# Reading the activations of a two-part float32 product in turn from four places

## The chip, the cores and the metric

The kernel runs on one core of one Trainium2 chip. The metric is the device time of one execution in microseconds (us). The kernel before takes 2208.91 us, the median of three runs (2207.38 to 2209.27).

## The reference

One inference step of a one-layer decoder trunk for a prompt of 256 tokens and 8 samples of 4 tokens, 288 tokens in all, of width 2048, in float32. Cut to what matters here:

```python
def swiglu(x, w_in, w_out):
    gate, up = jnp.split(x @ w_in, 2, axis=-1)
    return (jax.nn.silu(gate) * up) @ w_out
...
x = x + 0.5 * rmsnorm(swiglu(rmsnorm(x, g[0]), ffn1_w_in[l], ffn1_w_out[l]), g[1])
m, sg, sh = hybrid_mixer(rmsnorm(x, g[2]), mix_w_in[l], ...)   # merged @ mix_w_out inside
x = x + rmsnorm(m, g[3])
x = x + 0.5 * rmsnorm(swiglu(rmsnorm(x, g[4]), ffn2_w_in[l], ffn2_w_out[l]), g[5])
```

The FFNs are 5632 wide. The mixer projects its input to the operands of two groups of gated recurrences (GLA with 4 heads, HGRN2 with 8), runs them over chunks with exact causality, and projects the gated, normalised outputs back. Nearly all of the arithmetic is in products of the 288 tokens with the weight matrices.

## The kernel before

**Layout.** Everything is kept with features on the 128 partitions and the 288 tokens along the free axis, so x is 16 tiles of 128 x 288. A weight product holds a 128 x 128 slice of weights in TensorE and streams the 288 columns of an x tile past it into a PSUM tile.

**Two parts.** A float32 value is kept as a high part, which is the value rounded to the type `float32r` that TensorE multiplies in one pass, and a low part, which is the rest. A product of two values is then three products of parts: high x high, low x high and high x low. That is `mm3` in `block` (line 587 on): line 596 streams the high part of the activations past the high part of the weights, line 597 streams the low part past the same high slice, and line 598 streams the high part again past the low slice. All three add up in one PSUM tile. The helper that makes a matmul also makes the load of its slice of weights, so every product has a load of its own, line 597's too.

**The weights.** `Weights` (line 41 on) streams them. A unit is 512 KB, 128 x 1024 numbers: two rows of 128 features by 512 columns (in some products four by 256). `load` (line 65) issues its DMA on SyncE's queue into one of three `raw` buffers. `pieces` (line 86 on) splits it: ScalarE copies it to the high part (line 100), VectorE subtracts to get the low part (line 101). Both parts of a unit lie in one `wh` tile of two rows. A row holds 512 high numbers, then 512 low ones, then 32 numbers that nobody uses: `HALF` is 1024 + 32. Four such buffers (and two more at the borders between sub-layers) let the split run ahead of TensorE. `ahead` and `next` do this by counting; there is no planner.

**The loops.** `block` computes 512 (or 256) output features, as 4 PSUM tiles (`f`). It takes the units one after the other, and for each unit goes over `f`, over the unit's rows `k`, and over the three products. In some blocks at the beginnings of sub-layers (`byk`, `late`, `fill`) the order is by `k` first, with the products of the low part of the activations put later, because those parts are made while the block runs. TensorE executes in the order written.

**The activations' parts.** Those of x are `xh[k]` and `xl[k]` (lines 251 and 252), 32 tiles of 128 x 288. They are written by `split_to` (line 261): ScalarE writes the high part with a gain (line 262), VectorE the low part (line 263). The mixer writes its gated outputs into the same tiles in `split_y` (line 1637). At the two borders between sub-layers, `Fill` (line 513 on) has tiles of its own for the first four `k`, so that the next block's first products can begin before the norm is known.

In an FFN, `do_in` (line 667) computes a chunk of 512 hidden features: gate, up, and the activated product `u`. `ev_up` (line 689) writes the parts of `u` into `hh` and `hl`, two tiles of 128 x 4 x 288 each with two buffers (lines 693 and 694). `do_out` multiplies them with the second matrix; its `block` asks for `[t[:, k % 4, :] for t in hs[k // 4]]` (line 801). A result is read from PSUM by VectorE or ScalarE in the order of the tokens.

**Order around the change.** Engines wait for each other by semaphores that the framework derives from the tiles which instructions write and read. In a few places an order is written by hand with `tc.issue_after` and `order`, mostly at the borders: the post-norm's updates of x (line 566 on), the splits that follow each of them, and the first products that use them.

Of the kernel before, what the change touches and what calls it, by code (L numbers as in the profile page):

```python
# [9 lines left out]
F32 = mybir.dt.float32  # L10
F32R = mybir.dt.float32r
U8 = mybir.dt.uint8
AF = mybir.ActivationFunctionType
ALU = mybir.AluOpType
PSUM = bass.MemoryType.PSUM

P = 128
TP = 256
TS = 32
T = TP + TS  # L20
# [3 lines left out]
KT = D // P  # L24
# [8 lines left out]
HL_BUFS = 4  # L33
HALF = 1024 + 32
SCAN_LAG = 4
# [95 lines left out]
def trunk_kernel(ctx, tc, x_prompt, x_sample, state_gla, state_hgrn, norm_gains, f1_in, f1_out, f2_in, f2_out,  # L131
# [3 lines left out]
    V, S, G, PE = nc.vector, nc.scalar, nc.gpsimd, nc.tensor  # L135

    const = ctx.enter_context(tc.tile_pool(name="const", bufs=1))
    xpool = ctx.enter_context(tc.tile_pool(name="xpool", bufs=1))
# [108 lines left out]
    EARLY = 4  # L247
    x = [xpool.tile([P, T], F32, name=f"x{k}") for k in range(KT)]
    yg = [xpool.tile([P, 4, T], F32, name=f"y{k}") for k in range(4)]
    y = [yg[k // 4][:, k % 4, :] for k in range(KT)]  # L250
    xh = [xpool.tile([P, T], F32R, name=f"xh{k}") for k in range(KT)]
    xl = [xpool.tile([P, T], F32R, name=f"xl{k}") for k in range(KT)]
    rt = xpool.tile([P, T], F32, name="rt")
# [6 lines left out]

    def split_to(parts, src, col):
        i1 = S.activation(parts[0], src, AF.Copy, scale=col).ins
        i2 = V.scalar_tensor_tensor(parts[1], src, col, parts[0].bitcast(F32), op0=ALU.mult, op1=ALU.subtract).ins
        return i1, i2
# [246 lines left out]
    class Fill:  # L511
# [3 lines left out]
        def __init__(self, pool, name, gains, gnext, some, ahead):  # L515
            self.gnext, self.name, self.some, self.ahead = gnext, name, some, ahead

            tiles = [[[pool.tile([P, T], F32R, name=f"{name}{n}{p}{k}") for k in range(EARLY)] for p in "hl"] for n in "xy"]
            self.tiles = [list(zip(*hl)) for hl in tiles]
            self.gains = pool.tile([P, 48], F32, name=f"{name}g")[:, 0:EARLY]  # L520
            V.tensor_tensor(self.gains, gains[:, 0:EARLY], prm[:, gnext * KT:gnext * KT + EARLY], op=ALU.mult)
# [65 lines left out]
    def block(name, nk, rhs, evac, width=512, tick=None, tail=1, hold=False, most=99, fill=None, late=0, byk=(), lag=0, skip=()):  # L587
# [6 lines left out]
        def mm3(dst, w, f, k, parts, start, stop):  # L594
            a, c = k % per, slice(f * P, f * P + P)
            yield lambda: PE.matmul(dst, w[0][:, a, c], parts[0], start=start, stop=False)  # L596
            yield lambda: PE.matmul(dst, w[0][:, a, c], parts[1], start=False, stop=False)  # L597
            yield lambda: PE.matmul(dst, w[1][:, a, c], parts[0], start=False, stop=stop)  # L598
# [60 lines left out]
    def ffn(tag, gcol, gnext, pn, before, fill=None):  # L659
# [3 lines left out]
        with ExitStack() as pools:  # L663
# [3 lines left out]
            def do_in(c):  # L667
                hh = fp.tile([P, 4, T], F32R, name=f"hh{tag}_{c}", tag="hh")
                hl = fp.tile([P, 4, T], F32R, name=f"hl{tag}_{c}", tag="hl")
                hid[c] = (hh, hl)  # L670
# [18 lines left out]
                def ev_up(f, ps):  # L689
                    u = fp.tile([P, T], F32, name="u", tag="u", bufs=3)  # L690
                    ins = V.tensor_tensor(u, ps, rt, op=ALU.mult).ins  # L691
                    V.tensor_tensor(u, u, gs[f], op=ALU.mult)
                    S.activation(hh[:, f, :], u, AF.Copy)
                    V.tensor_tensor(hl[:, f, :], u, hh[:, f, :].bitcast(F32), op=ALU.subtract)
                    return ins
# [63 lines left out]
            def do_out(c, n):  # L759
                hs = [hid.pop(c + i) for i in range(n)]  # L760
# [7 lines left out]
                for o in range(4):  # L768
                    def ev(f, ps):
# [17 lines left out]
                        if end:  # L787
                            if not final:
                                border[0].fill.new(k)
                            elif k < KT - 1:  # L790
# [6 lines left out]
                                else:  # L797
                                    if f > 1:
                                        by_token(zs[f - 2], k - 2, *zt)
                                    zs.append(z)  # L800
                    block(f"out{tag}_{c}_{o}", 4 * n, lambda k: [t[:, k % 4, :] for t in hs[k // 4]], ev,
                          tail=2 if end and o == 3 else 1, hold=end and o == 3)
# [97 lines left out]
    def mixer(pn, border):  # L900
        with ExitStack() as mx:
# [735 lines left out]
            def split_y(t):  # L1637
                S.activation(xh[t], y[t], AF.Copy)
                V.tensor_tensor(xl[t], y[t], xh[t].bitcast(F32), op=ALU.subtract)

# [92 lines left out]
```

## Time and profile before

| What | Value |
|---|---|
| median of three runs | 2208.91 us |
| span of the profiled execution | 2206.5 us |
| TensorE busy, instructions | 2198.2 us, 17828 |
| VectorE busy | 1385.7 us (63%) |
| ScalarE busy | 1020.1 us (46%) |
| read from memory, written | 363.75 MB, 11.80 MB |
| mean rate of all transfers | 174 GB/s |

The profile is of one execution. PE is TensorE's matmuls, PEld its loads of weights, DVE is VectorE, ACT ScalarE, POOL GpSimd and SP SyncE, whose queue issues most DMAs. The span runs from the first to the last instruction of the program; the runs' times are of the whole execution. A group's row gives its line, engine, operation, what it writes and reads, its form and count, then the busy time, the mean duration in ns, and the time its engine sat idle just before, with what ended that. Matmuls are pipelined and their ends are modelled, so durations of neighbours overlap; their starts are recorded.

### The profile page before, as it was taken

To read this page: it belongs to the slowest core of one execution; us is meant where nothing else is said; L and a number is where in the kernel's file an instruction comes from. 1 tells how busy PE (TensorE), PEld (TensorE's weight loads), DVE (VectorE), ACT (ScalarE), POOL (GpSimd) and SP (SyncE) were. 2 spreads that over 40 slices of the span, in tenths; PEclk is the share of its full clock that TensorE was granted. 3 is DMA by queue.
4 is the path that set the end of the run, shared out by engine and by line. 5 is a ranking of instruction groups with operands and counts; after the bars stand their busy time and mean duration, and the time that the engine had idled before them with its cause. 6 is when DMAs were issued, how large, how long until landed. Compare 5 with 4: busy or idle time off the path is not lost.

```text
span 2206.5 us, 43225 instructions
## 1 busy us (share of the span) xinstructions
PE 2198.2 (100%) x17828; PEld 2182.2 (99%) x17828; DVE 1385.7 (63%) x2253; ACT 1020.1 (46%) x1537; POOL 180.0 (8%) x327
## 2 busy tenths in 40 slices
PE   9999999999999999999999999999999999999998
PEld 9999999999999999999999999999999999999998
DVE  7545546555555568888888755844555466556646
ACT  6443433343344345655676654543333333333344
POOL 2000000000000001233210000000000020122005
PEclk9999999999999999999999999999999999999999
DMA  7655555555555554667566564555555565666555
GB/s 223 174 166 171 169 168 170 171 165 171 172 166 180 179 166 142 194 207 216 173 189 176 176 190 135 169 167 171 171 166 170 172 176 172 180 179 179 172 164 161
DMA packets 227334, 384.87 MB, mean 174 GB/s; under 512 B 21362, under 2 KB 60864, under 8 KB 227136
## 3 DMA queue, kind: packets, MB, share of 16 engines
q1 hardware_dynamic: 213872, 365.02, 55.1%
q0 software_dynamic: 10992, 16.77, 2.8%
q8 instruction: 140, 2.29, 0.4%
q10 hardware_dynamic: 2272, 0.31, 0.1%
q14 instruction: 58, 0.48, 0.1%
HBM read 363.75 MB, written 11.80 MB: 170 GB/s over the span
## 4 chain that ended last, share of the span: by engine, by line
PE 98%; DVE 1%; ACT 1%; issue 0%; POOL 0%; DVEq 0%; ACTq 0%; POOLq 0%
PE gate L597 10%; PE gate L596 10%; PE gate L598 10%; PE up L597 8%; PE out L597 8%; PE up L596 8%; PE up L598 8%; PE out L596 8%; PE out L598 8%; PE hfq L596 2%; PE hfq L597 2%; PE mo L597 2%; PE hfq L598 2%; PE mo L596 1%; PE mo L598 1%; PE hi L597 1%
## 5 line engine op out<-in xcount | busy, mean ns | idle before, releaser
L101 DVE TENSOR_TENSOR wh<-raw,wh 128x1024 fp32r<-128x1024 f32 (+1 forms) x676 | 821.7, 1217 | 610.2 <-ACT wh L100 609.1
L100 ACT ACTIVATE wh<-raw 128x1024 fp32r<-128x1024 f32 (+1 forms) x676 | 711.0, 1053 | 943.1 <-PE gate L598 295.2
L597 PE MATMUL gate<-xl,wh 128*128 128x288 f32 x1660 | 490.1, 297 | 0.0
L598 PE MATMUL gate<-xh,wh 128*128 128x288 f32 x1660 | 483.6, 293 | 0.0
L596 PE MATMUL gate<-xh,wh 128*128 128x288 f32 x1660 | 483.0, 292 | 0.0
L597 PE MATMUL out<-hl,wh 128*128 128x288 f32 x1408 | 419.2, 298 | 0.0
L597 PE MATMUL up<-xl,wh 128*128 128x288 f32 x1408 | 419.2, 298 | 0.0
L598 PE MATMUL up<-xh,wh 128*128 128x288 f32 x1408 | 411.6, 292 | 0.0
L598 PE MATMUL out<-hh,wh 128*128 128x288 f32 x1408 | 411.5, 292 | 0.0
L596 PE MATMUL out<-hh,wh 128*128 128x288 f32 x1408 | 409.3, 291 | 0.0
L596 PE MATMUL up<-xh,wh 128*128 128x288 f32 x1408 | 409.3, 291 | 0.0
L596 PEld LDWEIGHTS gate<-xh,wh 128*128 128x128 f32 x1660 | 313.7, 189 | 0.8 <-DVE u L691 0.4
L598 PEld LDWEIGHTS gate<-xh,wh 128*128 128x128 f32 x1660 | 311.4, 188 | 0.2 <-DVE wh L101 0.2
L597 PEld LDWEIGHTS gate<-xl,wh 128*128 128x128 f32 x1660 | 310.2, 188 | 0.5
L596 PEld LDWEIGHTS out<-hh,wh 128*128 128x128 f32 x1408 | 266.8, 189 | 0.2 <-DVE y L782 0.2
L596 PEld LDWEIGHTS up<-xh,wh 128*128 128x128 f32 x1408 | 266.7, 189 | 0.0
L598 PEld LDWEIGHTS up<-xh,wh 128*128 128x128 f32 x1408 | 264.5, 188 | 0.0
L598 PEld LDWEIGHTS out<-hh,wh 128*128 128x128 f32 x1408 | 264.5, 188 | 0.0
L597 PEld LDWEIGHTS up<-xl,wh 128*128 128x128 f32 x1408 | 263.8, 187 | 0.0
L597 PEld LDWEIGHTS out<-hl,wh 128*128 128x128 f32 x1408 | 263.7, 187 | 0.0
L782 DVE TENSOR_TENSOR y<-out,y 128x288 f32<-128x288 f32 x287 | 120.7, 452 | 82.1 <-PE out L598 81.1
L739 POOL DMA_DIRECT2D xT<-b x64 | 37.1, 586 | 757.3 <-PE gate L598 566.7
(417 smaller groups left out, 2559.1 us busy)
## 6 DMA issues: line engine op xcount, KB each, us to landing
raw<-in_ffn_w_in_dram SPq DMA_DIRECT2D x350, 512.0 KB, 3.6
raw<-in_ffn_w_out_dram SPq DMA_DIRECT2D x176, 512.0 KB, 3.6
raw<-in_mix_w_in_dram SPq DMA_DIRECT2D x64, 512.0 KB, 4.3
raw<-in_mix_w_in_dram SPq DMA_DIRECT2D x96, 256.0 KB, 3.2
raw<-in_mix_w_out_dram SPq DMA_DIRECT2D x32, 512.0 KB, 3.7
out_dram<-s POOLq DMA_DIRECT2D x32, 256.0 KB, 2.9
s<-in_state_gla_dram SPq DMA_DIRECT2D x16, 256.0 KB, 5.9
s<-in_state_hgrn_dram SPq DMA_DIRECT2D x16, 256.0 KB, 5.6
```

What stands on the lines that cost most here:

```text
L100: i1 = self.nc.scalar.activation(h[:, a, c], raw[:, a, c], AF.Copy).ins
L101: i2 = self.nc.vector.tensor_tensor(l[:, a, c], raw[:, a, c], h[:, a, c].bitcast(F32), op=ALU.subtract).ins
L596: yield lambda: PE.matmul(dst, w[0][:, a, c], parts[0], start=start, stop=False)
L597: yield lambda: PE.matmul(dst, w[0][:, a, c], parts[1], start=False, stop=False)
L598: yield lambda: PE.matmul(dst, w[1][:, a, c], parts[0], start=False, stop=stop)
L739: queues[n % len(queues)].dma_start(dst[q * TS:(q + 1) * TS, 4 * g:4 * g + 4, :, cols].rearrange("p k t c -> p (k t) c"), b32[rows, q])
L782: V.tensor_tensor(y[k], ps, y[k], op=ALU.add)
```

## The change

The high and the low part of an activation tile now share one tile, made by a new function `pair`: 4 groups, in each group 72 high numbers and then 72 low ones. A group is a quarter of the tokens. `xh`, `xl`, the tiles of `Fill`, and `hh` and `hl` of an FFN chunk (now one tile `hp` of 4 such pairs) are views of these. Writers put the parts in through a view of the source in four groups (`columns`). In `mm3` both the streamed part and the PSUM tile are viewed through `turns_of`: the stream takes columns 0 to 3 of group 0, then 0 to 3 of group 1, of group 2, of group 3, then columns 4 to 7 of each, and so on for 18 rounds. A token's result still lands in the PSUM column of that token, so whatever reads PSUM is as before. The 32 unused numbers at the end of a row of `wh` go away.

```diff
-HALF = 1024 + 32
+HALF = 1024
+LINE = 4
+PLACES = 4
+
+
+def columns(t):
+
+    return t.rearrange("p (g c) -> p g c", g=PLACES)
+
+
+def turns_of(t):
+
+    return t.rearrange("p g (i e) -> p i g e", e=LINE)
+
+
+def pair(pool, name):
+
+    t = pool.tile([P, PLACES, 2, T // PLACES], F32R, name=name)
+    return t[:, :, 0, :], t[:, :, 1, :]
...
-    xh = [xpool.tile([P, T], F32R, name=f"xh{k}") for k in range(KT)]
-    xl = [xpool.tile([P, T], F32R, name=f"xl{k}") for k in range(KT)]
+    xh, xl = zip(*(pair(xpool, f"xp{k}") for k in range(KT)))
...
     def split_to(parts, src, col):
+        src = columns(src)
         i1 = S.activation(parts[0], src, AF.Copy, scale=col).ins
...
-            tiles = [[[pool.tile([P, T], F32R, name=f"{name}{n}{p}{k}") for k in range(EARLY)] for p in "hl"] for n in "xy"]
-            self.tiles = [list(zip(*hl)) for hl in tiles]
+            self.tiles = [[pair(pool, f"{name}{n}{k}") for k in range(EARLY)] for n in "xy"]
...
             a, c = k % per, slice(f * P, f * P + P)
+            dst, parts = turns_of(columns(dst)), [turns_of(t) for t in parts]
             yield lambda: PE.matmul(dst, w[0][:, a, c], parts[0], start=start, stop=False)
...
-                hh = fp.tile([P, 4, T], F32R, name=f"hh{tag}_{c}", tag="hh")
-                hl = fp.tile([P, 4, T], F32R, name=f"hl{tag}_{c}", tag="hl")
+                hp = fp.tile([P, 4, PLACES, 2, T // PLACES], F32R, name=f"hp{tag}_{c}", tag="hp")
+                hh, hl = ([hp[:, f, :, j, :] for f in range(4)] for j in range(2))
...
-                    S.activation(hh[:, f, :], u, AF.Copy)
-                    V.tensor_tensor(hl[:, f, :], u, hh[:, f, :].bitcast(F32), op=ALU.subtract)
+                    S.activation(hh[f], columns(u), AF.Copy)
+                    V.tensor_tensor(hl[f], columns(u), hh[f].bitcast(F32), op=ALU.subtract)
...
-                    block(f"out{tag}_{c}_{o}", 4 * n, lambda k: [t[:, k % 4, :] for t in hs[k // 4]], ev,
+                    block(f"out{tag}_{c}_{o}", 4 * n, lambda k: [t[k % 4] for t in hs[k // 4]], ev,
...
-                S.activation(xh[t], y[t], AF.Copy)
-                V.tensor_tensor(xl[t], y[t], xh[t].bitcast(F32), op=ALU.subtract)
+                S.activation(xh[t], columns(y[t]), AF.Copy)
+                V.tensor_tensor(xl[t], columns(y[t]), xh[t].bitcast(F32), op=ALU.subtract)
```

## The prediction

> **What bounds the kernel now.** I read the page first: the busy line, the granted clock and the chain that ended last.
>
> ```profile
> span 2206.5 us, 43225 instructions
> PE 2198.2 (100%) x17828; PEld 2182.2 (99%) x17828; DVE 1385.7 (63%) x2253; ACT 1020.1 (46%) x1537; POOL 180.0 (8%) x327
> PEclk9999999999999999999999999999999999999999
> PE 98%; DVE 1%; ACT 1%; issue 0%; POOL 0%; DVEq 0%; ACTq 0%; POOLq 0%
> ```
>
> TensorE is never out of work and its clock is granted in full; 98% of the chain is matmuls. Ends of matmuls overlap, so "100%" says only that there is always one in flight. What counts is how fast they follow each other. I take that from the busy time by stages, and for each of the three lines that issue a product (`hi x hi` L596, `lo x hi` L597, `hi x lo` L598) over the whole span and in the mixer. The columns are: stage, its length, TensorE busy (count), weight loads busy (count), then, where they are given, VectorE and ScalarE.
>
> ```profile
> 100.00:300.00 200.00, 200.00 (x1541) 200.00 (x1540) 106.67 (x141) 81.43 (x101) 0.00 (x0) 1.00 0.56 169
> 800.00:1300.00 500.00, 499.42 (x4813) 487.16 (x4812) 411.15 (x860) 307.33 (x627) 88.94 (x158) 1.00 0.63 184
> 1500.00:2150.00 650.00, 650.00 (x5003) 650.00 (x5002) 363.76 (x513) 249.36 (x282) 45.85 (x80) 1.00 0.57 172
> 0.00:2207.00 2207.00, 1568.05 (x5384) 1018.15 (x5384) 1.00 0.58 174
> 0.00:2207.00 2207.00, 1594.82 (x5384) 1007.35 (x5384) 1.00 0.58 174
> 0.00:2207.00 2207.00, 1572.69 (x5384) 1011.01 (x5384) 1.00 0.58 174
> 800.00:1300.00 500.00, 318.40 (x1083) 203.84 (x1083) 1.00 0.63 184
> ```
>
> In an FFN stretch a matmul starts every 650/5003 = 0.130 us. There are 3 x 5384 = 16152 products of 288 columns; at 130 ns they fill 2100 us of the span's 2206.5, so 1 ns on each is 16.2 us, or 0.73%. Of the products, 3 x 1083 = 3249 lie in the mixer stage (800 to 1300 us), the only long one where VectorE is also close to full (411 of 500 us); 12903 lie elsewhere.
>
> Next, whether the three products are alike. First the page's groups (count, busy, mean ns of one, idle before), then the order in time (start, duration), in two places because starts are rounded to 10 ns.
>
> ```profile
> L597 PE MATMUL out<-hl,wh 128*128 128x288 f32 x1408 | 419.2, 298 | 0.0
> L598 PE MATMUL out<-hh,wh 128*128 128x288 f32 x1408 | 411.5, 292 | 0.0
> L596 PE MATMUL out<-hh,wh 128*128 128x288 f32 x1408 | 409.3, 291 | 0.0
> ```
>
> ```profile
> 1417.64 0.29 PE L596 MATMUL up<-xh,wh 128*128 128x288 f32 x1
> 1417.76 0.30 PE L597 MATMUL up<-xl,wh 128*128 128x288 f32 x1
> 1417.90 0.29 PE L598 MATMUL up<-xh,wh 128*128 128x288 f32 x1
> 1418.03 0.29 PE L596 MATMUL up<-xh,wh 128*128 128x288 f32 x1
> ...
> 499.91 0.29 PE L596 MATMUL out<-hh,wh 128*128 128x288 f32 x1
> 500.04 0.30 PE L597 MATMUL out<-hl,wh 128*128 128x288 f32 x1
> 500.17 0.29 PE L598 MATMUL out<-hh,wh 128*128 128x288 f32 x1
> 500.30 0.29 PE L596 MATMUL out<-hh,wh 128*128 128x288 f32 x1
> ```
>
> They are not alike. The gap after L596 reads 0.12 in one place and 0.13 in the other, so it lies between 120 and 130 ns; the gap after L597 reads 0.14 and 0.13, so between 130 and 140; L598 takes the rest of the 390. Middles: 125, 135, 130. The durations say the same: 298 against 291. Shape, type, PSUM target and queue are equal and none waits (idle 0.0). What differs is what is read: while L596 streams, the load that follows it fetches the slice of weights just used, L597 again taking `w[0]`; behind L597 and L598 comes another slice. So 5 to 10 ns of the 130 hang on what TensorE reads from SBUF beside the stream. That is the only part of a matmul that this change can reach.
>
> **The change, part by part.** *Order of the stream.* No matmul, load or column is added or taken away. Each of the 16152 products reads 18 rounds of four columns from four places 576 bytes apart, instead of 1152 bytes in one run, and writes PSUM in the same rounds. By the code's sizes, counted in units of 256 bytes only to compare them, an x tile grows from 1152 bytes (4.5 x 256) to a pair of 2304 (9 x 256), a row of weights shrinks from 4224 to 4096, and the four places are 2.25 x 256 apart, so the stream meets four different residues in every round where it used to walk through them one after another. No row here shows what that does. Bounds from the nearest rows: if it takes from each matmul the whole difference between L597 and L596, 298 - 291 = 7 ns, the gap is 123 and the kernel gains 16152 x 7 = 113 us; if it gives every product the gap that follows L597, it loses 5 x 16152 = 81 us. I take the value between that a row already shows, L596's middle: **125 ns for all three, 5 ns less**. Outside the mixer that is 12903 x 5 = 64.5 us. In the mixer VectorE is busy 82% of the time and TensorE's next operands come from it, so I keep half: 3249 x 5 / 2 = 8.1 us. Together 72.6.
>
> By the Trainium skill ("TensorE: Matmul & The Clock Gate", Back-to-back issue gap) a warm matmul follows the last after N/2.4 + 2.5 ns, which is 122.5 for 288 columns; the trace has 130, and by the rule up to 7.5 x 16152 = 121 us, an estimate, could be had. It does not say what takes the 7.5.
>
> *Writes of the parts.* ScalarE and VectorE write high and low in four pieces of 72.
>
> ```profile
> L693 ACT ACTIVATE hh<-u 128x288 fp32r<-128x288 f32 x88 | 37.4, 445 | 58.1 <-DVE u L692 57.8
> L262 ACT ACTIVATE xh<-x,prm 128x288 fp32r<-128x288 f32 x36 | 18.0, 531 | 18.7 <-DVE x L568 16.9 <-DVE x L350 1.8
> L694 DVE TENSOR_TENSOR hl<-u,hh 128x288 fp32r<-128x288 f32 x88 | 37.9, 451 | 0.1
> L263 DVE SCALAR_TENSOR_TENSOR xl<-x,prm,xh 128x288 fp32r<-128x288 f32 x36 | 17.5, 514 | 0.8 <-ACT xh L262 0.6
> 842.09 0.55 ACT xh L262
> 842.68 0.40 PE qk L596
> ```
>
> Nothing shows a write in pieces; between forms of such a split 445 and 531 ns are seen, so I bound it at 0 to 86 ns each. Some 170 on each engine make at most 15 us, which TensorE's stream covers (VectorE 37% idle, ScalarE 54%). Without cover it costs on the chain: at the two borders between sub-layers, where the last split (842.09) ends as the first product that needs it starts (842.68). There 86 ns for up to 16 tiles on two engines are 2.8 us a border. *High and low in one tile.* If the high part's readers also had to wait for the low part's writer, L596, and with it all of TensorE behind it, since its products issue in order, would wait 514 ns a tile at a border: at most 16 x 0.51 = 8 us, and each block's evacuation, hence its next gate, comes that much later. Mostly the next tile's split runs on meanwhile. For both I take 1 us a border, 2 us; bounds 0 and 22.
>
> *The supply of weights* is read as before, but has to keep up with a faster consumer.
>
> ```profile
> L101 DVE TENSOR_TENSOR wh<-raw,wh 128x1024 fp32r<-128x1024 f32 (+1 forms) x676 | 821.7, 1217 | 610.2 <-ACT wh L100 609.1
> L100 ACT ACTIVATE wh<-raw 128x1024 fp32r<-128x1024 f32 (+1 forms) x676 | 711.0, 1053 | 943.1 <-PE gate L598 295.2
> GB/s 223 174 166 171 169 168 170 171 165 171 172 166 180 179 166 142 194 207 216 173 189 176 176 190 135 169 167 171 171 166 170 172 176 172 180 179 179 172 164 161
> ```
>
> A unit of 512 KB feeds 24 products: 3.12 us now, 3.0 us at 125 ns. VectorE's 1.22 and ScalarE's 1.05 us fit, 175 GB/s are needed where 223 were reached, and ScalarE waits for TensorE to free a buffer, not the other way. Cost nothing; without that cover it would be a stall for the difference of the two periods.
>
> *Sum*: 2206.5 - 72.6 + 2 = 2135.9 us of span. The profiled execution's span is 2.4 us under the median of the runs, 2208.9, which I add back: **2138 us**.
>
> **The rivals.** *A, no change.* The price is the load of a new slice itself, not a meeting of two reads: the order of the stream is then all one and 390 ns stay. For it: ScalarE and VectorE read and write the same memory all the time, and no product waits longer for it. The Trainium skill ("SBUF — State Buffer", Specifications) counts lines of 16 bytes and asks for two hits in each; four columns of 4 bytes fill one line, so by it the new order costs nothing and brings nothing, and the trace can't tell. Against it: L596 to L597 the same engine loads the same count of columns and is 10 ns cheaper. Time: 2209, within 2204 to 2213.
>
> *B, slower.* The place is the gap after L596. It is short because what is read there beside the stream suits a stream in one run; a stream that visits all four places in every round meets the load everywhere, and L596 pays what L597 pays: 5384 x 10 = 54 us, 2263. It decides from a mean gap of 130.3 ns. For it: two of the three gaps are already at 130 or above; against it: a round also leaves each place after four columns, so a meeting there is short.
>
> *C, slower still: PSUM.* A write that is broken into 72 runs costs something per break. Rows with two runs against one, in scores of 32 columns:
>
> ```profile
> L1120 PE MATMUL sc<-rp,one 128*32 128x32 f32 x96 | 2.2, 201 | 0.0
> L1205 PE MATMUL sc<-R,k_h 128*32 128x32 f32 x64 | 1.3, 201 | 0.0
> ```
>
> L1120 reads and writes two runs of 16, L1205 one run of 32: 201 and 201 ns, so no cost of a break to the nanosecond, though with one break, not 71. Rounded to half a nanosecond it could be up to 0.5 x 71 = 36 ns; already 0.1 ns a break is 7 ns, 115 us, 2324. The Trainium skill ("PSUM — Partial Sum Buffer", Specifications) says any pattern that is not contiguous slows matmuls significantly; by it this is the outcome, and the two rows speak against "any".
>
> *D, in part.* Only L597 and L598's surplus over 130 goes or comes down a little, 128 to 129.7 ns: 5 to 32 us, 2177 to 2204.
>
> **How the numbers follow.** The forecast, gaps of 123 to 128 and so 2095 to 2177, has 0.58; D 0.12; A 0.10; B 0.15; C 0.05. About 0.2%, 4.4 us, is what a measurement of this kernel can tell from no change. Faster is then 0.70, same 0.10, slower 0.20. The predicted time is the forecast's, 2138; its own range is 2095 (the 7 ns everywhere, 113 us) to 2177. The whole range goes on through D and A and a third of the way into B, to 2225, with the 22 us of border waits inside it; outside stay the rest of B, C, and what is gained beyond 7 ns, about 0.19 together.
>
> **What would show it.** Right: in 1500 to 2150 us some 5200 matmuls instead of 5003 (650/0.125); the three lines' durations come together; starts 0.12 to 0.13 apart in both places; VectorE and ScalarE groups longer by less than 86 ns with the supply's waits still ending at TensorE; the mixer stage shorter by about 8 us only. A shows the same 5003 and 298/291. B shows L596 at 298, C all three lines longer by the same. Waits of L596 for a writer of a low part would show the joint tile. The prediction is wrong if the gap stays at 130 or above, or if it falls and the span doesn't, which would mean a stage bound by another engine that I took for covered.

## The result, and the profile after

The changed kernel takes **2190.57 us**, the median of four runs, against 2208.38 us for the kernel before on the same chip: a ratio of **0.988, 95% interval 0.985 to 0.991**. It is faster, by 18 us at the medians, where 70 were forecast. Its runs lie far apart, 2164.24, 2185.01, 2196.12 and 2199.88, while those of the kernel before stay within 2 us. The ratio leaves out runs that are over 1.5% above the fastest of their kernel, which 2199.88 is, although its slowness turns out to be the program's own; the medians alone give 0.992.

The profiled execution is the one of 2185.01 us. First its page: span, busy times, the chain.

```profile
span 2183.2 us, 43224 instructions
PE 2174.0 (100%) x17828; PEld 2155.0 (99%) x17828; DVE 1384.0 (63%) x2253; ACT 1018.5 (47%) x1537; POOL 180.0 (8%) x327
PE 92%; DVE 3%; DMA 2%; ACT 1%; issue 1%; SPq 0%; POOL 0%; ACTq 0%; DVEq 0%; POOLq 0%
```

TensorE is as full as before, with the same 17828 matmuls. A stage in each FFN of the kernel before, then the same two of the changed one (stage, length, TensorE busy and count, loads, VectorE, ScalarE):

```profile
100.00:600.00 500.00, 500.00 (x3848) 500.00 (x3847) 272.63 (x365) 195.43 (x229) 0.00 (x0) 1.00 0.56 169
1500.00:2100.00 600.00, 600.00 (x4618) 600.00 (x4617) 338.32 (x481) 228.03 (x256) 45.85 (x80) 1.00 0.58 173
```

```profile
100.00:600.00 500.00, 500.00 (x3949) 500.00 (x3948) 277.90 (x373) 200.06 (x237) 0.00 (x0) 1.00 0.58 173
1500.00:2100.00 600.00, 600.00 (x4631) 600.00 (x4630) 338.94 (x482) 230.17 (x258) 45.83 (x80) 1.00 0.59 173
```

Stage length over count is the gap between starts. Before it is 500/3848 = 129.9 ns in the first FFN and 600/4618 = 129.9 in the second. After it is 500/3949 = **126.6** in the first and 600/4631 = **129.6** in the second: two nearly identical pieces of code, one of which gained 3.3 ns and the other 0.3. (A few matmuls in flight at a stage's edge are counted twice, so a gap reads about 0.1 ns short.) The page's groups for the three products:

```profile
L616 PE MATMUL out<-hp,wh 128*128 128x288 f32 x1408 | 410.6, 292 | 0.0
L615 PE MATMUL out<-hp,wh 128*128 128x288 f32 x1408 | 409.0, 290 | 0.3 <-DVE y L801 0.3
L617 PE MATMUL out<-hp,wh 128*128 128x288 f32 x1408 | 407.6, 289 | 0.0
```

The low part's product has come from 298 to 292 ns, the third from 292 to 289, and the first, the short one, only from 291 to 290. (These durations end at modelled ends; gaps between starts, product by product, stand further down.) In order of time, first FFN and then second (start, duration):

```profile
340.35 0.29 PE L615 MATMUL out<-hp,wh 128*128 128x288 f32 x1
340.47 0.29 PE L616 MATMUL out<-hp,wh 128*128 128x288 f32 x1
340.60 0.29 PE L617 MATMUL out<-hp,wh 128*128 128x288 f32 x1
340.73 0.29 PE L615 MATMUL out<-hp,wh 128*128 128x288 f32 x1
...
1601.21 0.30 PE L615 MATMUL out<-hp,wh 128*128 128x288 f32 x1
...
1601.61 0.29 PE L615 MATMUL out<-hp,wh 128*128 128x288 f32 x1
...
1601.99 0.29 PE L615 MATMUL out<-hp,wh 128*128 128x288 f32 x1
```

Three products take 0.38 us in the first place. In the second they take 0.40 and then 0.38: a beat that repeats over several products, where the kernel before had 0.39 each time. The first FFN keeps its 380 ns from 65 to 694 us. Then something interrupts it. The chain of waits that ended last in the changed kernel, just before that point (start, length):

```profile
687.18 4.83 DMA raw<-in_ffn_w_out_dram
692.11 1.07 ACT wh L119
693.21 1.23 DVE wh L120
```

And its timeline behind it (start, duration):

```profile
695.01 0.19 PEld L617 LDWEIGHTS out<-hp,wh 128*128 128x128 f32 x1
695.14 0.29 PE L617 MATMUL out<-hp,wh 128*128 128x288 f32 x1
695.22 0.19 PEld L615 LDWEIGHTS out<-hp,wh 128*128 128x128 f32 x1
695.26 0.36 PE L615 MATMUL out<-hp,wh 128*128 128x288 f32 x1
...
701.22 0.40 PE L615 MATMUL out<-hp,wh 128*128 128x288 f32 x1 [0.32 <-DVE y L801]
```

A load of weights that otherwise starts with the product before it (695.01) comes 80 ns after that product's start (695.22 against 695.14), and its own product takes 0.36 us. The chain runs through a transfer of 4.83 us and a unit's split just before, so a late unit of weights is the likely reason, though no row names what that load waited for. The chain goes on through VectorE's work, and a second, longer stop follows: the product before the last row starts at 700.61, so 0.61 us pass between two starts that are usually 0.13 apart, and the row names VectorE's reading of a result (`y` L801) as what ended the wait. The kernel before stops near this point too, for 0.31 us:

```profile
717.71 0.40 PE L596 MATMUL out<-hh,wh 128*128 128x288 f32 x1
```

After the two stops the three products no longer take 380 ns, although tiles, addresses and instructions are of the same kind. The stages add up to the gain: 630 us at 129.9/126.6 save 16. In the mixer, the products that start at 850.02 and 1250.06 us in the kernel before start at 833.39 and 1229.23 in the changed one, which is 4.2 us less between them. Some 930 us from there on at 0.3% are 2.6: together some 23 of the 23.3 us by which the span fell.

### The profile page after: what moved, and what is told of

Read it like the earlier page. It is cut to its first block, busy times and chain, and to the rows that moved or that the text cites. A ratio compares the mean times of both kernels' runs of the same rounds, so it can differ in the third digit from the quotient of the medians.

```text
span 2183.2 us, 43224 instructions
## 1 busy us (share of the span) xinstructions
PE 2174.0 (100%) x17828; PEld 2155.0 (99%) x17828; DVE 1384.0 (63%) x2253; ACT 1018.5 (47%) x1537; POOL 180.0 (8%) x327
## 4 chain that ended last, share of the span: by engine, by line
PE 92%; DVE 3%; DMA 2%; ACT 1%; issue 1%; SPq 0%; POOL 0%; ACTq 0%; DVEq 0%; POOLq 0%
PE gate L616 10%; PE gate L615 9%; PE gate L617 9%; PE out L616 8%; PE out L615 8%; PE up L616 8%; PE out L617 8%; PE up L615 8%; PE up L617 8%; PE mo L616 2%; PE mo L615 2%; PE mo L617 2%; PE hfq L615 1%; PE hfq L616 1%; PE hfq L617 1%; DVE wh L120 1%
## 5 line engine op out<-in xcount | busy, mean ns | idle before, releaser
L615 PE MATMUL gate<-xp,wh 128*128 128x288 f32 x1660 | 481.9, 292 | 0.2
L616 PE MATMUL gate<-xp,wh 128*128 128x288 f32 x1660 | 480.8, 292 | 0.5 <-DVE xp L282 0.4
L617 PE MATMUL gate<-xp,wh 128*128 128x288 f32 x1660 | 477.9, 289 | 0.0
L616 PE MATMUL out<-hp,wh 128*128 128x288 f32 x1408 | 410.6, 292 | 0.0
L616 PE MATMUL up<-xp,wh 128*128 128x288 f32 x1408 | 410.5, 292 | 0.0
L615 PE MATMUL out<-hp,wh 128*128 128x288 f32 x1408 | 409.0, 290 | 0.3 <-DVE y L801 0.3
L615 PE MATMUL up<-xp,wh 128*128 128x288 f32 x1408 | 408.9, 290 | 0.0
L617 PE MATMUL out<-hp,wh 128*128 128x288 f32 x1408 | 407.6, 289 | 0.0
L617 PE MATMUL up<-xp,wh 128*128 128x288 f32 x1408 | 407.1, 289 | 0.0
L615 PEld LDWEIGHTS gate<-xp,wh 128*128 128x128 f32 x1660 | 311.2, 188 | 1.1 <-issue 0.3
L616 PEld LDWEIGHTS gate<-xp,wh 128*128 128x128 f32 x1660 | 310.2, 188 | 1.6 <-DVE xp L282 1.3
L617 PEld LDWEIGHTS gate<-xp,wh 128*128 128x128 f32 x1660 | 311.1, 188 | 0.2 <-DVE wh L120 0.2
L615 PEld LDWEIGHTS out<-hp,wh 128*128 128x128 f32 x1408 | 264.6, 188 | 0.6 <-DVE y L801 0.5
L615 PEld LDWEIGHTS up<-xp,wh 128*128 128x128 f32 x1408 | 264.3, 188 | 0.0
L617 PEld LDWEIGHTS up<-xp,wh 128*128 128x128 f32 x1408 | 264.2, 188 | 0.1
L617 PEld LDWEIGHTS out<-hp,wh 128*128 128x128 f32 x1408 | 264.3, 188 | 0.0
L616 PEld LDWEIGHTS out<-hp,wh 128*128 128x128 f32 x1408 | 264.0, 188 | 0.0
L616 PEld LDWEIGHTS up<-xp,wh 128*128 128x128 f32 x1408 | 264.0, 188 | 0.0
L801 DVE TENSOR_TENSOR y<-out,y 128x288 f32<-128x288 f32 x287 | 119.7, 452 | 79.2 <-PE out L617 78.7
```

Source lines behind the costliest of these rows:

```text
L801: V.tensor_tensor(y[k], ps, y[k], op=ALU.add)
```

## The experiments

All results below are medians with the 95% interval of the ratio to the kernel before, which ran beside each. The row shown is the second FFN's stage; the gap is its length over the count of matmuls.

**What of the change counts.** Three kernels take it apart.

Pairs and short rows, but in the order of the tokens:

```diff
-            dst, parts = turns_of(columns(dst)), [turns_of(t) for t in parts]
+            dst = columns(dst)
```

> The changed kernel, but the stream and PSUM go in the order of the tokens (four runs of 72 columns); the joint tiles and the rows of 1024 stay. Theory 1, the order of the stream brings the gain: three products take about 390 ns again (130 each), about 2208 us, or a little more, since the weights' rows have lost the 32 numbers that set them apart from the x tiles. Theory 2, the new places of the tiles bring it: 380 to 389 ns for three as in the changed kernel, 2165 to 2200 us.

```profile
1500.00:2100.00 600.00, 600.00 (x4552) 600.00 (x4552) 331.03 (x466) 228.21 (x262) 45.84 (x80) 1.00 0.57 171
```

2232.85 us, ratio 1.011 (1.009 to 1.012), gap 600/4552 = 131.8. The layout alone makes the kernel slower, so the gain is the order's, and the order has to make good a loss first.

Turns on the old tiles (high and low apart, rows of 1056):

```diff
-    t = pool.tile([P, PLACES, 2, T // PLACES], F32R, name=name)
-    return t[:, :, 0, :], t[:, :, 1, :]
+    return tuple(columns(pool.tile([P, T], F32R, name=f"{name}{j}")) for j in "hl")
...
-                hp = fp.tile([P, 4, PLACES, 2, T // PLACES], F32R, name=f"hp{tag}_{c}", tag="hp")
-                hh, hl = ([hp[:, f, :, j, :] for f in range(4)] for j in range(2))
+                hps = [fp.tile([P, 4, T], F32R, name=f"hp{j}{tag}_{c}", tag=f"hp{j}") for j in "hl"]
+                hh, hl = ([columns(hp[:, f, :]) for f in range(4)] for hp in hps)
```

> The tiles of the kernel before (high and low apart, weight rows of 1056 numbers) with the changed order: the four places are 288 bytes apart instead of 576. Theory 1, turns alone suffice: 2165 to 2200 us. Theory 1b, the places must differ by a quarter of 256 bytes, which 576 (2.25 x 256) gives and 288 (1.125 x 256) doesn't: 385 ns or more for three, 2190 to 2215 us. Theory 2, places of tiles alone: as the kernel before, 390 ns, 2208 us.

```profile
1500.00:2100.00 600.00, 600.00 (x4558) 600.00 (x4557) 330.68 (x467) 228.85 (x262) 45.83 (x80) 1.00 0.57 171
```

2233.50 us, 1.011 (1.009 to 1.012), gap 131.6. Turns over places 288 bytes apart are a loss; turns over places 576 bytes apart are a gain (128.1 with the same rows of weights, further down). That is what the joint tile is for: it sets the groups 2.25 x 256 bytes apart. (That the tiles as such also lie elsewhere is not told apart from this.) The "385 ns or more" of the expectation covers its 394 for three, but not the time, which was to end at 2215 us; that it would be a loss was not foreseen.

The write to PSUM in one run:

```diff
-            dst, parts = turns_of(columns(dst)), [turns_of(t) for t in parts]
+            parts = [turns_of(t) for t in parts]
+            dst = dst.rearrange("p (i g e) -> p i g e", g=PLACES, e=LINE)
```

> The changed kernel, but a product's result is written to PSUM in one run, in the order in which the columns are read; a token's result lands in another token's column, so this leaves out putting the tokens back in order. If the gain is in the read and breaks in the PSUM write are free (theory 1): 2165 to 2200 us as the changed kernel, the same few patterns of three. If broken PSUM writes ate the missing part of the gain (the rival that names PSUM): patterns below 379 ns for three, about 125 each, 2130 to 2150 us.

```profile
1500.00:2100.00 600.00, 600.00 (x4631) 600.00 (x4630) 338.78 (x482) 228.82 (x257) 45.85 (x80) 1.00 0.58 174
```

2186.67 us, 0.991 (0.987 to 0.994), and 4631 matmuls, to the matmul what the changed kernel has in this stage. The 71 breaks in the PSUM write cost nothing that shows. The rest of the gain was not lost there.

**Where the weights lie.** First the kernel before without the unused numbers:

```diff
-HALF = 1024 + 32
+HALF = 1024
```

> The kernel before without the 32 unused numbers in the weights' rows, nothing else. If the pairs' loss in token order (2233 us) came from the rows: 395 ns for three, 2230 us or more. If it came from the pairs themselves: 390 ns, 2208 us.

```profile
1500.00:2100.00 600.00, 600.00 (x4541) 600.00 (x4539) 326.64 (x460) 228.73 (x262) 45.83 (x80) 1.00 0.57 170
```

2238.60 us, 1.014 (1.012 to 1.016), gap 132.1. Moving every second row of weights by 128 bytes, with nothing else changed in the code, is worth 2.2 ns a product. So the gap depends on where the weights lie, too, and most of the layout's loss in the first experiment came with the short rows.

Then the changed kernel with longer rows, `HALF = 1024 + 32`, `+ 16`, `+ 48` and `+ 8`:

> The changed kernel with the weights' rows at 1056 numbers again, so that of a unit's two rows one is shifted by 128 bytes against the stream. If a stream in turns meets the load the same wherever that begins: the same patterns, 2165 to 2200 us. If the relation of addresses still counts: another set of patterns, every second slice different, outside 379 to 381 for a pair of triples.

```profile
100.00:600.00 500.00, 500.00 (x3905) 500.00 (x3903) 274.38 (x368) 197.73 (x231) 0.00 (x0) 1.00 0.57 171
1500.00:2100.00 600.00, 600.00 (x4684) 600.00 (x4683) 341.66 (x484) 232.86 (x264) 45.87 (x80) 1.00 0.59 176
```

> The changed kernel with rows of 1040 numbers: a unit's two rows are shifted by 64 bytes against each other, a quarter of 256. With a shift of 0 the kernel has several patterns (2164 to 2200 us), with 128 one pattern of 384 ns for three (2179). Theory, the shift breaks up a beat between the stream and the load: one steady pattern here too, between 378 and 388, 2155 to 2190 us, runs within 3 us. Rival, the shift of 128 was a lucky one: several patterns and runs 15 us or more apart.

```profile
1500.00:2100.00 600.00, 600.00 (x4652) 600.00 (x4652) 340.14 (x483) 229.56 (x258) 45.86 (x80) 1.00 0.58 174
```

> The changed kernel with rows of 1072 numbers, a shift of 192 bytes between a unit's two rows. Shifts so far: 0 gives several patterns, 64 one of 387 ns for three, 128 one of 384. If the shift counts modulo 128 in effect, or alike in both directions: 387 and 2192 us as with 64. If it counts as a distance along the stream: something else, 380 to 384, at or below 2179 us.

```profile
1500.00:2100.00 600.00, 600.00 (x4672) 600.00 (x4672) 342.79 (x487) 233.38 (x264) 45.88 (x80) 1.00 0.59 175
```

> The changed kernel with rows of 1032 numbers, a shift of 32 bytes between a unit's two rows. Shifts of 64, 128 and 192 bytes gave steady gaps of 129.0, 128.15 and 128.5 ns, a shift of 0 two or three patterns from 126.67 up. If any shift breaks up the patterns: one steady gap between 127 and 129.5, 2162 to 2200 us, runs within 3 us. If shifts below a quarter of 256 bytes leave the patterns alone: runs 10 us or more apart.

```profile
1500.00:2100.00 600.00, 600.00 (x4650) 600.00 (x4649) 340.31 (x482) 228.82 (x258) 46.01 (x80) 1.00 0.58 175
```

| Shift between a unit's rows | Gap, second FFN | Time | Runs apart by |
|---|---|---|---|
| 0 (the changed kernel) | 129.6 | 2190.57 | 36 us |
| 32 bytes | 129.0 | 2192.93 | 1.9 |
| 64 bytes | 129.0 | 2191.87 | 1.5 |
| 128 bytes | 128.1 | 2179.07 | 1.0 |
| 192 bytes | 128.4 | 2183.97 | 1.5 |

Each of the four shifts makes the runs agree. With 128 bytes both FFNs have one gap, 500/3905 = 128.0 and 600/4684 = 128.1, and the time is 0.986 (0.985 to 0.988) of the kernel before. 192 bytes gave neither of the two times that its expectation allowed, 2192 us as with 64, or 2179 and less.

The low half of a row moved by another 64 bytes, at rows of 1056:

```diff
-        h, l = hl[:, :, 0:512], hl[:, :, 512:1024]
+        h, l = hl[:, :, 0:512], hl[:, :, 528:1040]
```

> The changed kernel with rows of 1056 numbers, and the low half of a row 64 bytes further on, so that of three products the third product's load lies a quarter of 256 bytes off the other two. If a beat between stream and load sets the gap, more different starts mean shorter meetings: 380 to 383 for three, 2160 to 2175 us, steady. If only the shift between rows counts: 384 and 2179 us. If it makes things worse: up to 390, 2208 us.

```profile
1500.00:2100.00 600.00, 600.00 (x4684) 600.00 (x4683) 342.31 (x486) 233.10 (x263) 45.88 (x80) 1.00 0.59 176
```

2180.04 us, 0.987 (0.986 to 0.989), gap 128.1: the same as with the row's shift alone. More different starts do not shorten it.

**How many places, and how long at each.** At rows of 1056, `PLACES = 2`, then `LINE = 8`:

> The changed kernel with rows of 1056 numbers and two groups of 144 tokens instead of four of 72; the two places are 1152 bytes apart (4.5 x 256), so a stream alternates between two of four quarters of 256 bytes and then moves on. If all four quarters must be visited in a round: worse than 128.15 ns (2179 us), about 130 to 132, 2208 to 2235 us. If any leaving of a place after four columns is enough: 128 ns, 2179 us.

```profile
1500.00:2100.00 600.00, 600.00 (x4357) 600.00 (x4356) 308.49 (x423) 225.06 (x259) 34.48 (x60) 1.00 0.54 163
```

2327.00 us, 1.053 (1.051 to 1.055), gap 600/4357 = 137.7: by far the worst, 5% slower than the stream in one run, and worse than either theory allowed. Alternating between two places 4.5 x 256 bytes apart is no half-way house to four.

> The changed kernel with rows of 1056 numbers and turns of eight columns (32 bytes of each place) instead of four. If a meeting costs more the longer the stream stays in one place: between the stream in one run (390 or more) and turns of four (384), about 386 to 390, 2190 to 2210 us. If the length of a turn does not count as long as all four places are visited: 384, 2179 us.

```profile
1500.00:2100.00 600.00, 600.00 (x4578) 600.00 (x4578) 334.26 (x473) 228.32 (x259) 45.85 (x80) 1.00 0.58 172
```

2223.48 us, 1.007 (1.005 to 1.008), gap 131.1. Eight columns at each of the four places lose the whole gain; with 393 for three this is more than the expectation allowed.

**Patterns that keep themselves up.** The changed kernel again, unchanged:

> The changed kernel itself, unchanged, for a second profile. Theory: a stretch of work that nothing interrupts keeps the pattern of gaps that it came into, and which one that is turns on small chances at an interruption; the first FFN (380 ns for three in the first profile) and the second (386 to 389) then need not have the same patterns as before, and the new runs lie anywhere between 2155 and 2205 us, at least 10 us apart. Rival: a pattern belongs to a place of the program; then the first FFN has 380 again and the second 386 to 389.

```profile
100.00:600.00 500.00, 500.00 (x3949) 500.00 (x3949) 277.48 (x372) 200.79 (x237) 0.00 (x0) 1.00 0.57 173
1500.00:2100.00 600.00, 600.00 (x4631) 600.00 (x4630) 339.16 (x481) 230.12 (x258) 45.86 (x80) 1.00 0.58 174
```

2181.00 us, 0.984 (0.978 to 0.990; the medians alone give 0.988), runs from 2161.90 to 2199.03. The first and the second FFN show 3949 and 4631 matmuls again, so in these two profiles the places kept their patterns, as the rival had it. But behind the interruption they differ. The same stretch in the first profile of the changed kernel and in this one:

```profile
702.00:815.00 113.00, 113.00 (x871) 113.00 (x871) 66.06 (x93) 48.58 (x61) 0.00 (x0) 1.00 0.56 174
```

```profile
702.00:815.00 113.00, 113.00 (x894) 113.00 (x893) 67.61 (x97) 49.17 (x63) 0.00 (x0) 1.00 0.58 177
```

871 matmuls in 113 us, a gap of 129.7, against 894 and 126.4. The second profile was interrupted as well, twice, and its pattern changed each time:

```profile
697.24 0.30 PE L615 MATMUL out<-hp,wh 128*128 128x288 f32 x1
...
697.64 0.29 PE L615 MATMUL out<-hp,wh 128*128 128x288 f32 x1
...
698.02 0.29 PE L615 MATMUL out<-hp,wh 128*128 128x288 f32 x1
...
700.81 0.40 PE L615 MATMUL out<-hp,wh 128*128 128x288 f32 x1 [0.29 <-DVE y L801]
```

A stop (0.41 us between two starts, at 694.41) ended the fast pattern: behind it the three products take 0.40 and 0.38 us by turns, as in the second FFN. Another (0.58 us, at 700.23) ended the slow one, and the 126.4 ns follow. And in the kernel with the write in one run, whose stream is the same, the first FFN has the slow pattern; so it has in the kernel of the next experiment, whose first FFN is the changed kernel's, instruction for instruction:

```profile
100.00:600.00 500.00, 500.00 (x3860) 500.00 (x3859) 272.80 (x365) 195.64 (x229) 0.00 (x0) 1.00 0.56 170
```

```profile
100.00:600.00 500.00, 500.00 (x3859) 500.00 (x3858) 272.89 (x365) 195.72 (x229) 0.00 (x0) 1.00 0.56 169
```

500/3860 = 129.5. So one and the same stream can run at 126.6 or 129.6, in the same place of the program, and the rival, that a pattern belongs to its place, falls too. In all four profiles TensorE stops at about 64 us, with 0.26 to 0.50 us between two starts; the changed kernel comes out of this stop with the fast pattern twice, the other two with the slow one. A kick was to show what changes it: an extra matmul of 64 columns at the start of some 50 blocks of the second FFN.

```diff
         ps = [mmtile(f"{name}_{f}") for f in range(nf)]
+        if name[:5] in ("gate2", "up2_1", ..., "up2_9", "out2_") and "_0" != name[-2:]:
+            PE.matmul(ps[0][:, 0:64], onesR, onesR[:, 0:64], start=True, stop=True)
```

> The changed kernel with one extra matmul of 64 columns at the start of some 50 blocks of the second FFN, whose sums the block's first product overwrites; it takes about 0.11 us each, 6 us in all, and shifts the stream against the loads. Theory: a pattern of gaps keeps itself up until something shifts the stream, so in the second FFN the pattern now changes from block to block between about 380, 386 to 389 and 390 for three, and the runs lie closer together than 2164 to 2200. Rival: the pattern belongs to the place in the program (addresses, what other engines do): the second FFN keeps one pattern, the same after each kick.

```profile
1500.00:2100.00 600.00, 600.00 (x4639) 600.00 (x4639) 338.23 (x480) 226.88 (x256) 45.83 (x80) 1.00 0.58 173
```

2202.92 us, 0.996 (0.994 to 0.998), and the slow pattern all through, 4639 with the kicks themselves among them. The kicks did not change it, against the theory, and the time is 12 us above the changed kernel's first median. Eight of its ten runs lie within 6 us, the other two 11 and 16 us below them. What is shown is that the patterns exist, that each lasts for hundreds of microseconds when nothing interrupts, and that in the first FFN they changed only where TensorE stopped. What picks the next one, and why a kick does not, is not settled.

**What the surplus is.** The kernel before with the high slice of weights in all three products:

```diff
-            yield lambda: PE.matmul(dst, w[1][:, a, c], parts[0], start=False, stop=stop)
+            yield lambda: PE.matmul(dst, w[0][:, a, c], parts[0], start=False, stop=stop)
```

> The kernel before, but the third product takes the high slice of the weights again instead of the low one (the product of the high part with the low weights is left out, one with the high weights stands in its place). Theory: a gap is short where the load beside the stream fetches the slice that is loaded already, whichever part streams; then the gap of the low part's product falls from 133 to about 126 ns too, three take 383 and the kernel 5384 x 7 = 38 us less, about 2171. Rival: the low part's stream itself is slow (its place in memory): its gap stays at 133, three at 390, 2208 us.

The groups of the FFNs' second matrix, for the second and the first product:

```profile
L597 PE MATMUL out<-hl,wh 128*128 128x288 f32 x1408 | 419.0, 298 | 0.0
L596 PE MATMUL out<-hh,wh 128*128 128x288 f32 x1408 | 408.7, 290 | 0.0
```

One run, 2206.93 us, and the durations are as before. A load that repeats the slice does not make the low part's gap short; the theory fell. (The two slices lie 2048 bytes apart, so the run says nothing of smaller shifts.)

Then the walks themselves, in the kernel before: the load on one number, the stream on one number, both; and the load on one number in the changed kernel.

```diff
+            parts = [t[:, 0:1].broadcast_to([P, T]) for t in parts]
...
-            yield lambda: PE.matmul(dst, w[0][:, a, c], parts[0], start=start, stop=False)
+            yield lambda: PE.matmul(dst, w[0][:, a, f * P:f * P + 1].broadcast_to([P, P]), parts[0], start=start, stop=False)
```

> The kernel before, but each load of a 128 x 128 slice reads its first column 128 times instead of 128 columns (the other columns of weights are left out); count of columns, products and everything else stay. If the surplus is the meeting of the stream with the load's walk: the gap leaves 130 ns, to 122 to 126, 64 to 130 us less, 2080 to 2145 us. If it is a fixed price of a product or of a load: 130 ns and 2208 us.

```profile
1500.00:2100.00 600.00, 600.00 (x4540) 600.00 (x4539) 328.46 (x462) 228.17 (x262) 45.99 (x80) 1.00 0.57 170
```

> The changed kernel with loads that stay on one number, as in the run beside it. If the surplus is the meeting of stream and load: one steady pattern, gap 122 to 126 ns, 2080 to 2145 us, and the order of the stream no longer matters, so within 10 us of the run beside it. If it is a fixed price: 126.7 or 129.6 ns by stretches as before, 2162 to 2200 us.

```profile
1500.00:2100.00 600.00, 600.00 (x4657) 600.00 (x4656) 342.08 (x486) 230.14 (x261) 45.84 (x80) 1.00 0.58 175
```

> The kernel before, but each product streams its first column 288 times (the other tokens' columns are left out); loads as they are. If the stream's walk through memory makes the surplus, alone or by meeting the load: the gap falls to 120 to 124 ns, 97 to 160 us less, 2050 to 2110 us. If the surplus is a fixed price of a product: 130 ns, 2208 us. If reading one place again and again is itself the slow case: above 132 ns, over 2240 us.

```profile
1500.00:2050.00 550.00, 550.00 (x4493) 550.00 (x4492) 325.77 (x470) 225.23 (x261) 45.87 (x80) 1.00 0.62 184
```

> The kernel before with the stream on one number and the load on one number as well. With nothing walking, the gap is what a product of 288 columns costs by itself: 120 to 124 ns if the surplus comes from walking, and the same as in the run beside it if the load plays no part; 130 ns or more if it is a fixed price.

```profile
1500.00:2050.00 550.00, 550.00 (x4492) 550.00 (x4492) 325.05 (x467) 224.78 (x259) 46.03 (x80) 1.00 0.61 184
```

| Kernel before | Load walks | Load on one number |
|---|---|---|
| stream walks in one run | 129.9 ns, 2208 us | 132.2 ns, 2236.74 us |
| stream on one number | 122.4 ns, 2099.08 us | 122.4 ns, 2099.34 us |

In the changed kernel with the load on one number the gap is 600/4657 = 128.8 ns and the time 2189.08 us. So the surplus over 122.4 is there when the stream walks and gone when it stands, whatever the load does. A load that stands still does not remove it; with it the gap is 132.2 where it was 129.9. The groups of the kernel before with the load on one number show which product loses:

```profile
L597 PE MATMUL out<-hl,wh 128*128 128x288 f32 x1408 | 416.8, 296 | 0.0
L596 PE MATMUL out<-hh,wh 128*128 128x288 f32 x1408 | 415.4, 295 | 0.0
```

It is the first, which goes from 291 to 295 ns. The recorded starts, averaged over the stages above, say it more sharply. Mean gap after each of the three products, in ns:

| Kernel | high x high | low x high | high x low |
|---|---|---|---|
| before | 125.8 | 133.4 | 130.8 |
| before, high slice in all three | 125.8 | 133.4 | 130.8 |
| before, load on one number | 132.5 | 133.3 | 130.8 |
| before, rows of 1024 | 131.7 | 132.5 | 132.5 |
| before, stream on one number | 122.5 | 122.5 | 122.5 |
| changed, first FFN (fast) | 127.1 | 127.9 | 125.0 |
| changed, second FFN (slow) | 129.4 | 131.1 | 128.3 |
| changed, load on one number | 130.8 | 126.2 | 129.6 |

In the kernel before the short gap does hang on the load: it goes when the load stands, while the other two gaps keep their size, and it goes when the rows lose their shift. The change does not spread it. It lengthens the short gap, by 1.3 or 3.6 ns, and shortens the other two. The changed layout and order are worth 3.4 ns (132.2 to 128.8) even against a load that stands. That the surplus needs two *walks* that meet, as the theory had it, is refuted. A stream on one number also carries the same value in every column; the granted clock is full in all these rows (the 1.00), so the clock is not how that could act, but place and value are not told apart by these runs. Whether a walking stream would pay without any load beside it stays open, since each product has its load.

## Why the prediction was wrong

**The step that failed is the size taken for a gap: 125 ns for all three products.** I took the gap that followed L596 as something the turns would give to every product. My middles were right to a nanosecond or two, 125, 135 and 130 against 125.8, 133.4 and 130.8. (The durations did not say the same: they put L598 1 ns above L596 where the gaps put it 5.) But the short gap was a third of a beat of 390 ns, and even L596 did not keep it: with the turns its gap is 127.1 or 129.4. Its reason, that it is short because the same slice is fetched again, was a reading of the code put beside the row, and the run with one slice in all three products speaks against it: the low part's gap stays at 133.4. What came in place of the 125 is 126.6 ns in the first FFN and 129.6 in the second; from 1500 to 2150 us there are 5017 matmuls where I had some 5200. Why the turns save what they save stays open: no run says what in the addresses makes a gap. Outside the mixer I had 64.5 us for 5 ns on all 12903 products; the FFNs gave 16 where 3.3 ns were gained and under 3 where 0.3 were.

**That the order of the stream is the lever, and no fixed price stands in its way, was right.** Rival A needed 390 ns to stay whatever is read; the gap moved from 126.6 to 137.7 with nothing but addresses and order changed. My ground for it was half right: the short gap depends on the load beside the stream, but the surplus is there without the load's walk (132.2 ns) and gone without the stream's (122.4).

**Rivals.** D, "128 to 129.7 ns, 2177 to 2204 us", with 0.12, is what happened at the median: the two long gaps come down, as it had it. In the time it is a mixture of two patterns, and in one of them the gain goes beyond D's. B had the short gap grow to 135. It does grow, to 129.4 at most, but the other two together fall by more. Two places gave 137.7; whether by B's mechanism is not shown. C is out: 71 breaks in PSUM cost nothing that shows. The Trainium skill ("PSUM — Partial Sum Buffer", Specifications) has any pattern that is not contiguous slow a matmul significantly; with runs of four columns these runs do not bear that out.

**The covered parts were costed rightly.** The changed kernel's rows for the splits:

```profile
L712 ACT ACTIVATE hp<-u 128x288 fp32r<-128x288 f32 x88 | 37.5, 445 | 58.6 <-DVE u L711 57.7
L281 ACT ACTIVATE xp<-x,prm 128x288 fp32r<-128x288 f32 x36 | 18.0, 531 | 19.2 <-DVE x L586 17.4 <-DVE x L369 1.8
```

And of its waits, the one for a low part of x (total, times, longest, in us):

```profile
PEld gate L616 <- DVE xp L282: 1.3, 4, 0.6
```

445 and 531 ns, to the nanosecond as before: four pieces cost a write nothing. Of the 1.3 us that the low part's product waited here for its operand's writer, 0.8 fall at the program's start and 0.5 at the second border; at the first it waited 0.5, and the first product 0.6 for its own writer. That is 1.6 us at the two borders, where the kernel before has 0.6 and I took 2 more. No row has the first product wait for the writer of a low part, which would have shown the joint tile. The supply was covered but for moments: the stops at 695 and 701 us cost well under 1 us in themselves, and the kernel before has one too, but the fast pattern ended there, a price that no row of the kernel before could show. In the mixer I kept half of the saving as a guess; it gave 4.2 us over 400 where I had 8.1 over 500.

**The range** ended at 2095 and 2225 and holds the time, but by the parts for D and A; the forecast's own range, 2095 to 2177, does not. The chance of faster, 0.70, was on the right side. The lower end took the whole 298 - 291 = 7 ns off every matmul; 3.3 ns came in one FFN and 0.3 in the other. By the Trainium skill ("TensorE: Matmul & The Clock Gate", Back-to-back issue gap) the gap of an isolated warm matmul of 288 columns is 288/2.4 + 2.5 = 122.5 ns; the trace agrees, with 122.4, where the stream stands, and with no stream that walks. Such a number says how much there may be to win, not how much of it a change gets.

Whether any version beats the changed kernel's median is not sure. Rows of 1056 in the changed kernel give 2179.07 us against 2190.57 and 2181.00 for the changed kernel in two sets of runs; what is sure is that its runs agree within 1.0 us where the other's lie 36 apart.

## What to carry to other kernels

When TensorE never waits and its clock is full, divide a steady stage by its count of matmuls and compare that with the same kernel whose stream is held on one number: the difference (7.5 ns of 129.9 here) is what streaming from changing places costs, or changing values, which that run does not tell apart, and it says how much there may be to win. Then try the layouts on the chip, a few at a time: distances between groups, turn lengths and row lengths changed the gap from 126.6 to 137.7 ns here with no rule that foretold it. A gap that is short for one product of three is no price to forecast for all three. A spread between runs can be the program's own, and a profile shows only one of its patterns; a layout with one steady pattern is easier to build on than one with a faster best run.

## What the runs showed of the hardware that was not expected

- A stream of 288 `float32r` columns has a gap of 122.4 ns when it reads one place and 129.9 to 132.2 in one run. In turns of four columns over four places 576 bytes apart it has 126.6 to 129.6, over places 288 bytes apart 131.6, over two places 1152 bytes apart 137.7.
- Moving every second row of weights by 128 bytes changes the gap from 132.1 to 129.9 in one program and from 126.6 or 129.6 to a steady 128.1 in another.
- The same stream in the same place ran at 126.6 ns in one program and at 129.5 in two others, of which one differs only in the order of its PSUM writes and the other only in a later stage, each for some 500 us on end; runs of one program lay 36 us apart with a full clock. In the first FFN the pattern changed only where TensorE stopped, with 0.2 to 0.6 us between two starts, and in either direction.
- With the load of weights on one number the first product's gap went from 125.8 to 132.5 ns, while those of the second and the third stayed within 0.1 ns.
- Writing PSUM in 72 runs of four columns is as fast as in one run (4631 matmuls in 600 us either way).
